# Output projections of two token groups in one pass over their weights, a weight ring of four whole blocks, and the first two block products taken two at once

## The chip, the core and the metric

The kernel runs on one core of a Trainium2 chip. The core has five engines: PE (TensorE) multiplies matrices, DVE (VectorE) and ACT (ScalarE) work on tiles of 128 partitions, POOL (GpSimd) does tile work that needs no PSUM, and SP (SyncE) issues most of the loads. The engines run side by side, each works its own list in order, and they wait for one another by semaphores. The metric is the device time of one execution in microseconds (us); lower is better.

## The reference, cut to what matters

One inference step of a hybrid decoder with two layers: layer 0 mixes tokens with a causal convolution, layer 1 with the RWKV-7 recurrence; each is followed by an MLP with a squared ReLU. The model width is 1024, the MLP's is 4096. There are 1040 prompt tokens (16 of them meta tokens) and 8 decode tokens, 1048 columns in all, in float32.

```python
def _sqrelu_mlp(h, w_in, w_out):
    return jnp.square(jax.nn.relu(h @ w_in)) @ w_out
...
def _rwkv7(h, shift_prev, S0, x_mix, w_r, w_k, w_v, w_o, ...):
    ...
    S_final, ys = lax.scan(_wkv7_step, S0.astype(f32), xs)
    ...
    out = ((yn + bonus).astype(h.dtype) * g) @ w_o
    return out, h[:, -1], S_final.astype(S0.dtype)
...
def _trunk(h, ...):
    for i in range(DEPTH):
        hn = _rmsnorm(h, norm_mix[i])
        ...
        h = h + out
        h = h + _sqrelu_mlp(_rmsnorm(h, norm_mlp[i]), w_mlp_in[i], w_mlp_out[i])
    return (_rmsnorm(h, norm_final), ...)
```

The change touches `out = (...) @ w_o` of layer 1, and the beginning of layer 1's MLP.

## The kernel before

**A matmul is three.** Every dense product is made from `float32` operands that are cut into a high part, rounded to the fast format `fp32r`, and the low rest. `mm3` issues high x high, low weight x high activation, and high weight x low activation (lines 190 to 192). For a weight block of 128 partitions x 1024 columns, ACT makes the high part (a CAST, line 158) and POOL subtracts it from the raw block in four pieces of 256 columns to get the low part (line 165). Both stand between the load and PE. For an activation tile ACT casts and DVE (or POOL) subtracts (lines 141 and 142).

**Token groups.** Layer 1's columns are worked in three groups: group 0 has 328 columns, groups one and two (the second and the third) have 352 each. `wide` is 352. Group two holds the decode tokens too, so its input `z2` needs the end of `decode_step`, which is worked beside group 0's MLP.

**Output projection.** `mixer_out(g)` loads the group's `z`, cuts it, and loops over the 8 column blocks `m` of `w_o`: the product `oo{g}_{m}` is 24 matmuls (8 pieces of the inner dimension times three), then DVE adds it to the residual `h1` (line 1685), ACT squares the sum (line 273), and POOL or DVE gathers the squares (`acc_m`, line 284) for the next norm. Weights are asked for two blocks ahead. For group 0 a weight block is one pair of tiles out of a pool of 5 (`lf`, closed after group 0's MLP). For groups one and two a block is two half-block `unit`s out of a ring of 8 halves (`units`), so four blocks; each group loads, casts and subtracts all 8 blocks. Raw blocks land in tiles of tag `raw`.

**Side work.** While PE runs a list, `fill()` advances generators between its products. Group 0's list has the tail of the recurrence (its chunk state `fs`, lines 1308 and 1426), the decode step and the group norms as side work; group one's has `final(0)` (sums `acc_f`, their matmul `fs` at line 1706, transposes `pf` at line 1722); group two's has `later_half`, which makes the norm of group one (`st_m` at line 262, a reciprocal, eight `nf` at line 1798) and the first half of the activations of the block products.

**Block products.** The MLP of groups one and two together is a seven-product scheme of the Strassen kind over pairs `s` of MLP blocks. Its products are named "1" to "7"; each is 4 pieces x 3 = 12 matmuls into one of the banks V, Z, X, Y. "7" goes to Z, "3" to Y in the first two pairs, "1" and "2" to V and X. `weight(s, q)` makes the operand of product `q`, for most by DVE additions of quarter blocks (the tiles `s` of pool `mixw`). "7" and "3" need only group one's activations (`b2`), the others need group two's norm as well (`first_half`). The first two pairs, `s` = 0 and 1, are worked in an order of their own; the rest in steady turns with the second MLP matmul (`out`).

**What sets the order.** PE's list is in program order inside `in_order()`; the other engines' lists are ordered by the framework's scheduler with its own timeline, so a change at one place can move rows of DVE, ACT and POOL elsewhere. SBUF is handed out from stacked pools: a tile of a new pool waits for the last users of the address that it takes.

Of the kernel before, what the change touches and what calls it, by code (L numbers as in the profile page):

```python
# [8 lines left out]
F32 = mybir.dt.float32  # L9
# [37 lines left out]
def hybrid_step(tc, x_prompt, x_sample, state_conv, state_shift, state_wkv, meta_tokens,  # L47
# [10 lines left out]
    with ctx:  # L58
# [91 lines left out]
        def load_w(src, shape, name, eng_lo, tag="w", raw=None, keep=False):  # L150
# [43 lines left out]
        UK, UB = KT // 2, 8  # L194
# [18 lines left out]
        def unit(src, name, keep=False):  # L213

            hi, lo = (cur["units"].tile([P, UK, P], F32R, name=f"{name}_{q}", tag="u" + q, bufs=UB) for q in "hl")
            a, b = src.shape[1:]
            hv, lv = (t.rearrange("p k c -> p (k c)").rearrange("p (a b) -> p a b", a=a) for t in (hi, lo))
# [6 lines left out]
            return (hi, lo) if b == P else (hv, lv)  # L224
# [40 lines left out]
        def square_sums(n, name, place, engs, own=False):  # L265
# [5 lines left out]
            def add(k, src):  # L271
# [7 lines left out]
                else:  # L279
                    a = b = out[i][:, :n] if i < len(out) else None  # L280
                    if a is None:
                        out.append(stat(f"acc_{name}{i}", f"acc{i}", 1))
                        a, b = out[i][:, :n], first[i]
# [1358 lines left out]
        with ExitStack() as l1:  # L1642
            open_tmp(l1, N2, "2", 3, False)
            actp = pool(l1, "actp1", 1)
# [3 lines left out]
            lf = ctx.enter_context(ExitStack())  # L1648
            open_weights(lf, 0, {"w": 5}, "f")
# [9 lines left out]
            def mixer_out(g, actp, fill, add):  # L1659
                lo, n = G2[g]  # L1660
                h1 = hl[g]

                def block(m):
                    if not g:
                        return load_col(rwkv_w_o[0], m, f"wo{g}_{m}", nc.gpsimd, keep=m > 0)
                    raw = blocks_of(load_raw(col_src(rwkv_w_o[0], m), (KT, P), f"wo{g}_{m}"))
                    return [unit(raw[:, i * UK:(i + 1) * UK], f"wo{g}_{m}_{i}", m > 0) for i in range(2)]
                z = new_acts(actp, f"z{g}", cur["wide"])
                ws, per = [], 8 * P // n
                for p in range(0, KT, per):  # L1670
# [4 lines left out]
                    if p == 0:  # L1675
                        ws.append(block(0))
# [3 lines left out]
                ws.append(block(1))  # L1680
                for m in range(KT):
                    if m + 2 < KT:
                        ws.append(block(m + 2))
                    ps = dense(ws.pop(0), z, n, f"oo{g}_{m}", fill)
                    nc.vector.tensor_add(h1[:, m, :n], h1[:, m, :n], ps[:, :n])
                    add(m, h1[:, m, :n])
# [340 lines left out]
```

## Time and profile before

| what | value |
|---|---|
| three runs | 2664.55, 2668.51, 2669.19 us, median 2668.51 |
| profiled execution | 2664.08 us, span 2662.3 us, 1.8 us outside the span |
| mean granted clock of PE | 0.987 |
| busy share of the span | PE 97%, DVE 68%, POOL 60%, ACT 45% |
| group 0's projection starts | 1701.5 us |
| projection of group one starts, group two's ends | 2068.2 us, about 2146.7 us |
| second MLP matmul starts | 2202.9 us |

The profiled execution is 4.4 us below the median of the three runs. In the profile's lists of waits a row names the engine that waits, what it wanted to do, and who released it. In a timeline a row has the start and the length in us, the engine, the line, the operation, what it writes and reads, how many such instructions in a row, and in brackets the idle time ahead of it and its releaser. In a table by stretches of time the last three columns are PE's granted clock as a share of full speed, the busy share of the DMA engines, and GB/s.

### The profile page before, as it was taken

The page shows a single profiled execution, that of the slowest core. Times are in us where ns is not written, and L with a number is a line of the kernel's source. Part 1 is how long each engine was busy: PE and PEld are TensorE (multiplying, and loading weights), DVE is VectorE, ACT ScalarE, POOL GpSimd, SP SyncE. Part 2 cuts the span into 40 slices and gives each one's busy share as a digit, 9 for nine tenths or more (in the row PEclk, how much of TensorE's full clock was granted, in tenths as well). Part 3 has the DMA queues.
Part 4 walks back from the last instruction along what each step waited for, and adds up shares of the span by engine and source line. Part 5 has one row for each costly group of instructions (what it writes and reads, how often), then busy time and mean ns, then how long its engine had stood idle before and what let it go on. Part 6 is the DMA issues. An engine that isn't in the chain of part 4 may idle for free.

```text
span 2662.3 us, 51898 instructions
## 1 busy us (share of the span) xinstructions
PE 2571.5 (97%) x19764; PEld 2422.5 (91%) x19764; DVE 1820.4 (68%) x3723; ACT 1187.7 (45%) x2264; POOL 1589.1 (60%) x2170
## 2 busy tenths in 40 slices
PE   8999999999999999999999999889999979999998
PEld 8999999999999999777788877789999869999998
DVE  6999999997444344445758567676689586565655
ACT  5546445444544333333345545454543543333333
POOL 7677878877878876022112113465587786666662
PEclk9999999999999999999999999899999999999999
DMA  7663544554446543678777858958665522222221
GB/s 188 171 170 107 166 140 133 159 178 135 136 140 186 155 136 111 201 202 220 209 185 204 219 145 215 236 143 191 174 193 172 149 69 72 64 80 80 64 72 44
DMA packets 602062, 400.24 MB, mean 150 GB/s; under 512 B 96128, under 2 KB 548928, under 8 KB 601814
## 3 DMA queue, kind: packets, MB, share of 16 engines
q1 hardware_dynamic: 573764, 360.08, 48.9%
q0 software_dynamic: 8720, 26.35, 3.3%
q10 hardware_dynamic: 19330, 10.49, 1.4%
q8 instruction: 156, 2.56, 0.4%
q14 instruction: 92, 0.75, 0.1%
HBM read 338.94 MB, written 58.83 MB: 149 GB/s over the span
## 4 chain that ended last, share of the span: by engine, by line
PE 80%; DVE 11%; DMA 3%; POOL 2%; ACT 2%; issue 2%; ACTq 0%; SPq 0%; DVEq 0%; POOLq 0%
PE out L190 8%; PE out L192 8%; PE out L191 8%; PE ps_in L190 5%; PE ps_in L191 5%; PE ps_in L192 5%; PE pk L943 4%; PE pr L943 4%; PE pv L943 3%; PE V L192 1%; PE V L190 1%; PE V L191 1%; PE ps_o L192 1%; PE ps_o L190 1%; PE ps_o L191 1%
## 5 line engine op out<-in xcount | busy, mean ns | idle before, releaser
L165 POOL TENSOR_TENSOR wo_lo<-wo_raw,wo_hi 128x256 fp32r<-128x256 f32 x544 | 397.9, 763 | 122.8 <-ACT wo_hi L158 117.2
L165 POOL TENSOR_TENSOR wi_lo<-wi_raw,wi_hi 128x256 fp32r<-128x256 f32 x512 | 378.0, 771 | 106.8 <-ACT wi_hi L158 103.0
L563 DVE SCALAR_TENSOR_TENSOR cv<-u,wdw,cv 128x348 f32<-128x348 f32 (+2 forms) x720 | 377.6, 574 | 0.7
L190 PE MATMUL out<-hh,wo_hi 128*128 128x348 f32 (+2 forms) x1024 | 332.3, 324 | 8.8 <-DVE h L381 7.4
L190 PE MATMUL ps_in<-m_h,wi_hi 128*128 128x348 f32 (+2 forms) x1024 | 328.7, 321 | 0.0
L192 PE MATMUL ps_in<-m_l,wi_hi 128*128 128x348 f32 (+2 forms) x1024 | 327.2, 320 | 0.5 <-DVE m_l L309 0.5
L191 PE MATMUL ps_in<-m_h,wi_lo 128*128 128x348 f32 (+2 forms) x1024 | 326.8, 319 | 0.0
L191 PE MATMUL out<-hh,wo_lo 128*128 128x348 f32 (+2 forms) x1024 | 326.7, 319 | 0.0
L192 PE MATMUL out<-hl,wo_hi 128*128 128x348 f32 (+2 forms) x1024 | 326.6, 319 | 0.0
L381 DVE TENSOR_TENSOR h<-h,out 128x348 f32<-128x348 f32 (+2 forms) x512 | 253.3, 505 | 69.5 <-PE out L192 67.8
L158 ACT CAST wi_hi<-wi_raw 128x1024 fp32r<-128x1024 f32 x128 | 134.1, 1048 | 260.2 <-PE ps_in L192 108.5
L158 ACT CAST wo_hi<-wo_raw 128x1024 fp32r<-128x1024 f32 x136 | 142.4, 1048 | 196.1 <-PE ps_in L192 91.9
L223 POOL TENSOR_TENSOR wo_l<-wo_raw,wo_h 128x256 fp32r<-128x256 f32 x192 | 163.7, 877 | 73.1 <-ACT wo_h L218 69.0
L190 PEld LDWEIGHTS out<-hh,wo_hi 128*128 128x128 f32 x1024 | 193.2, 189 | 14.1 <-DVE h L381 10.0
L190 PEld LDWEIGHTS ps_in<-m_h,wi_hi 128*128 128x128 f32 x1024 | 192.7, 188 | 1.3
L191 PEld LDWEIGHTS out<-hh,wo_lo 128*128 128x128 f32 x1024 | 192.5, 188 | 0.8
L192 PEld LDWEIGHTS ps_in<-m_l,wi_hi 128*128 128x128 f32 x1024 | 192.1, 188 | 1.1 <-DVE m_l L309 0.7
L191 PEld LDWEIGHTS ps_in<-m_h,wi_lo 128*128 128x128 f32 x1024 | 192.6, 188 | 0.5
L192 PEld LDWEIGHTS out<-hl,wo_hi 128*128 128x128 f32 x1024 | 192.3, 188 | 0.0
L1940 DVE TENSOR_TENSOR h<-h,out 128x352 f32<-128x352 f32 x256 | 131.7, 516 | 85.4 <-PE out L192 85.1
L192 PE MATMUL out<-hl,wo_h 128*128 128x352 f32 x512 | 167.3, 327 | 4.3 <-DVE hl L142 4.3
L190 PE MATMUL out<-hh,wo_h 128*128 128x352 f32 x512 | 167.6, 327 | 0.2 <-ACT hh L141 0.2
(475 smaller groups left out, 6685.8 us busy)
## 6 DMA issues: line engine op xcount, KB each, us to landing
wi_raw<-in_w_mlp_in_dram SPq DMA_DIRECT2D x160, 512.0 KB
wo_raw<-in_w_mlp_out_dram SPq DMA_DIRECT2D x160, 512.0 KB
wk_raw<-in_rwkv_w_k_dram SPq DMA_DIRECT2D x32, 512.0 KB
wr_raw<-in_rwkv_w_r_dram SPq DMA_DIRECT2D x32, 512.0 KB
wv_raw<-in_rwkv_w_v_dram SPq DMA_DIRECT2D x32, 512.0 KB
d_ab<-ab POOLq DMA_DIRECT2D x32, 512.0 KB, 4.3
pg_raw<-in_conv_w_pw_dram SPq DMA_DIRECT2D x24, 512.0 KB
pa_raw<-in_conv_w_pw_dram SPq DMA_DIRECT2D x24, 512.0 KB
```

Of the source, the lines that this page charges most:

```text
L158: cast = nc.scalar.copy(hi[:, :a * b], raw[:, :a * b])
L165: eng_lo.tensor_sub(lo[:, cs], raw[:, cs], hi[:, cs].bitcast(F32))
L190: nc.tensor.matmul(ps, w[0], act[0], start=first, stop=False, skip_group_check=onto)
L191: nc.tensor.matmul(ps, w[1], act[0], start=False, stop=False, skip_group_check=onto)
L192: nc.tensor.matmul(ps, w[0], act[1], start=False, stop=last, skip_group_check=onto)
L223: nc.gpsimd.tensor_sub(lv[:, i:i + step], src[:, i:i + step], hv[:, i:i + step].bitcast(F32))
L381: total = nc.vector.tensor_add(hv[:, 4 * i + m, :], hv[:, 4 * i + m, :], ps[:, :n])
L563: nc.vector.scalar_tensor_tensor(acc[m][:, :n], ug[:, m, j:j + n], wdw[:, m, j:j + 1], acc[m][:, :n], op0=ALU.mult, op1=ALU.add)
L943: nc.tensor.matmul(ps[:, :n], w[:, k, :], act[k], start=k == 0, stop=k == KT - 1)
L1940: nc.vector.tensor_add(hl[g][:, m, :n], hl[g][:, m, :n], ps[:, :n])
```

## The change

1. One loop takes the projections of groups one and two: `oo1_m`, and then `oo2_{m-3}` (`LEAD` = 3). Each block of `w_o` is loaded, cast and subtracted once and used by both groups: 8 loads of 512 KB, 8 blocks' casts and 32 subtractions fewer.
2. The weight ring is opened early, ahead of `actp1`, as two pools: `wspf` with four block slots and `wsps` with one. Group 0 goes round all five; from group one on the four are the ring, and the fifth's tiles become the quarter-block tiles of `weight`. A block-product `unit` is half of a slot's pair of tiles.
3. The first two pairs are worked two at once: `product("7", 0, 1)` alternates between the two banks piece by piece, in the order 7, 3, 1, 2, 6, 4, 5, with the weights of "7" and "3" of both pairs asked for first. Where two products alternate and their weights lie in one slot, the ring of four holds both.
4. The squared ReLU moves from one DVE operation to two ACT ones (Relu, Square), and works in PSUM. The reciprocal of the joint MLP's norms is written into PSUM.

The diff, cut:

```diff
@@ weights @@
-            nb = cur["bufs"][tag]
-            hi = cur["wsp"].tile([P, 8 * P], F32R, name=f"{name}_hi", tag=tag + "h", bufs=nb)
-            lo = cur["wsp"].tile([P, 8 * P], F32R, name=f"{name}_lo", tag=tag + "l", bufs=nb)
+            if "slot" in cur:
+                hi, lo = cur["slot"](name)
+            else:
...
         def unit(src, name, keep=False):
-            hi, lo = (cur["units"].tile([P, UK, P], F32R, name=f"{name}_{q}", tag="u" + q, bufs=UB) for q in "hl")
+            if not cur.get("pair"):
+                cur["pair"] = [t[:, i * UK * P:(i + 1) * UK * P] for t in cur["slot"](name) for i in range(2)]
+            hi, lo = cur["pair"].pop(0), cur["pair"].pop(len(cur["pair"]) // 2)
@@ layer 1 @@
             open_tmp(l1, N2, "2", 3, False)
+            rings = [pool(l1, f"wsp{i}", 1) for i in "fs"]
             actp = pool(l1, "actp1", 1)
...
-            lf = ctx.enter_context(ExitStack())
-            open_weights(lf, 0, {"w": 5}, "f")
+            cur["ring"], cur["turn"] = (0, 0, 0, 0, 1), 0
+            def slot(name):
+                i = cur["ring"][cur["turn"] % len(cur["ring"])]
+                cur["turn"] += 1
+                return [rings[i].tile([P, 8 * P], F32R, name=f"{name}_{q}", tag="w" + q, bufs=(4, 1)[i]) for q in ("hi", "lo")]
+            cur["slot"] = slot
...
-            lf.close()
             cur["wide"] = wide
-            cur["units"] = pool(l1, "units", UB)
-            mixed_w = pool(l1, "mixw", 5)
...
-            with in_order():
-                mixer_out(1, actp, fill, add)
...
+            cur["ring"] = (0,)
...
-            fill, rest = filler(2 * KT, ([late_start(2), later_half(sums)], 2 + 2 * UK + 2))
-            add, sums = sums_of(2)
+            LEAD = 3
+            adds = {}
+            fill, rest = filler(3 * KT, ([late_start(4), final(0)], FB + 4))
+            fills = {1: fill, 2: fill}
             with in_order():
-                mixer_out(2, actp2, fill, add)
+                for g in (1, 2):
+                    adds[g] = sums_of(g, ("rsm", 2) if g == 2 else None)
+                ws = {}
+                zs = {1: load_z(1, actp, lambda: ws.update({0: wo_block(0, "")}))}
+                for m in (1, 2):
+                    ws[m] = wo_block(m, "")
+                for m in range(KT + LEAD):
+                    if m < KT:
+                        if m + 3 < KT:
+                            ws[m + 3] = wo_block(m + 3, "")
+                        wo_product(1, m, ws[m], zs[1], fills[1], adds[1][0])
+                    if m == 0:
+                        zs[2] = load_z(2, actp2)
+                    if m == KT - 1:
+                        for _ in rest:
+                            pass
+                        fills[2], rest = filler(2 * LEAD + 2, ([late_start(1), later_half(adds[1][1])], 2 * UK + 1))
+                    if m >= LEAD:
+                        wo_product(2, m - LEAD, ws.pop(m - LEAD), zs[2], fills[2], adds[2][0])
...
             def squared(c):
-                nc.vector.scalar_tensor_tensor(c, c, 0.0, c, op0=ALU.max, op1=ALU.mult)
+                nc.scalar.activation(c, c, AF.Relu)
+                nc.scalar.activation(c, c, AF.Square)
...
                 for k in range(UK):
-                    mm3(ps, block_of([w], k), [t[k][:, :n] for t in hi_lo[q]], first and k == 0, k == UK - 1, not first)
+                    for s, w in zip(sets, ws):
+                        mm3(held[s, tag], block_of([w], k), [t[k][:, :n] for t in hi_lo[q]], first and k == 0, k == UK - 1, not first)
+                for s in sets:
+                    landed(s, q, early)
...
-                product(0, "7", True)
+                for s in range(2):
+                    ahead.update({(s, q): weight(s, q) for q in "73"})
+                product("7", 0, 1, early=True)
                 first_half(sums)
-                product(0, "3", True)
-                for q in "73":
-                    product(1, q, True)
...
+                for q in "3126":
+                    product(q, 0, 1, early=True)
+                for q in "45":
+                    product(q, 0, 1)
```

Here `wo_product` is the body of the old loop over `m`, and `load_z` its beginning.

How instructions move, at three places. In these rows a name's trailing number tells one tile from the next, and brackets hold the engines and DMA queues whose semaphores the instruction waits for. First PE, around group one's product for block 4, before:

```order
L190 MATMUL ps_oo_3_24377<-z_h_24116,wo_3_1_h 128x352
L191 MATMUL ps_oo_3_24377<-z_h_24116,wo_3_1_l 128x352
L192 MATMUL ps_oo_3_24377<-z_l_24124,wo_3_1_h 128x352
L190 MATMUL ps_oo_4_24433<-z_h_24109,wo_4_0_h 128x352 [waits Activation_49]
L191 MATMUL ps_oo_4_24433<-z_h_24109,wo_4_0_l 128x352 [waits Pool_49]
L192 MATMUL ps_oo_4_24433<-z_l_24117,wo_4_0_h 128x352
```

and after, where `ps_oo_0` is group two's product for block 0:

```order
L193 MATMUL ps_oo_0_24423<-z_h_24219,wo_hi 128x352
L194 MATMUL ps_oo_0_24423<-z_h_24219,wo_lo 128x352
L195 MATMUL ps_oo_0_24423<-z_l_24227,wo_hi 128x352 [waits DVE_49]
L193 MATMUL ps_oo_4_24474<-z_h_24108,wo_hi 128x352 [waits Activation_49]
L194 MATMUL ps_oo_4_24474<-z_h_24108,wo_lo 128x352 [waits Pool_49]
L195 MATMUL ps_oo_4_24474<-z_l_24116,wo_hi 128x352
```

The last reader of block 0's slot, which block 4 takes over, now stands directly in front of block 4's first reader.

Second POOL, in group 0's projection, where its sum `acc_m` takes the square of block 4, before:

```order
L284 TENSOR_TENSOR acc_m_19632<-acc_m_19632,sq_4_19767 128x328 [waits Activation_49,Pool_49]
L1274 MEMSET ni_19306 128x32 [waits DMAHW6_49,DVE_49]
L1275 DMA d_p<-ni_19306 128x1024 [waits DMASW7_49,DVE_49,Pool_49]
L165 TENSOR_TENSOR wo_7_lo<-wo_7_raw,wo_7_hi 128x256 [waits DMAHW1_49,PE_49,Activation_49]
L165 TENSOR_TENSOR wo_7_lo<-wo_7_raw,wo_7_hi 128x256 x3
L165 TENSOR_TENSOR wi_0_0_lo<-wi_0_0_raw,wi_0_0_hi 128x256 [waits DMAHW5_49,PE_49,Activation_49]
L165 TENSOR_TENSOR wi_0_0_lo<-wi_0_0_raw,wi_0_0_hi 128x256 x3
L165 TENSOR_TENSOR wi_0_1_lo<-wi_0_1_raw,wi_0_1_hi 128x256 [waits DMAHW6_49,PE_49,Activation_49]
L165 TENSOR_TENSOR wi_0_1_lo<-wi_0_1_raw,wi_0_1_hi 128x256 x3
L165 TENSOR_TENSOR wi_0_2_lo<-wi_0_2_raw,wi_0_2_hi 128x256 [waits DMAHW7_49,Activation_49]
```

and after:

```order
L168 TENSOR_TENSOR wi_0_1_lo<-wi_0_1_raw,wi_0_1_hi 128x256 [waits DMAHW6_49,Activation_49,Pool_49]
L168 TENSOR_TENSOR wi_0_1_lo<-wi_0_1_raw,wi_0_1_hi 128x256 x3
L289 TENSOR_TENSOR acc_m_19635<-acc_m_19635,sq_4_19770 128x328 [waits Activation_49,Pool_49]
L168 TENSOR_TENSOR wo_7_lo<-wo_7_raw,wo_7_hi 128x256 [waits DMAHW1_49,Activation_49]
L168 TENSOR_TENSOR wo_7_lo<-wo_7_raw,wo_7_hi 128x256 x3
L168 TENSOR_TENSOR wi_0_0_lo<-wi_0_0_raw,wi_0_0_hi 128x256 [waits DMAHW5_49,Activation_49]
L168 TENSOR_TENSOR wi_0_0_lo<-wi_0_0_raw,wi_0_0_hi 128x256 x3
L1279 MEMSET ni_19306 128x32 [waits DMAHW3_49,DVE_49]
L168 TENSOR_TENSOR wi_0_2_lo<-wi_0_2_raw,wi_0_2_hi 128x256 [waits DMAHW7_49,Activation_49]
```

The memset that waits for DVE has moved from ahead of the subtractions of `wo_7` and of the first three blocks of the MLP to between the second and the third of what is left of them. On ACT, the cast of group 0's block 0 moves from behind the eight `z_h` casts to ahead of them.

Third PE, at the norm of group one (`st_m`), before, in group two's block 1:

```order
L191 MATMUL ps_oo_1_24684<-z_h_24571,wo_1_0_l 128x352
L192 MATMUL ps_oo_1_24684<-z_l_24579,wo_1_0_h 128x352
L262 MATMUL st_m_24697<-acc_m_24363,ones_d 128x352
L262 MATMUL st_m_24697<-acc_m_24419,ones_d 128x352
L262 MATMUL st_m_24697<-sq_6_24529,ones_d 128x352 [waits Activation_49]
L262 MATMUL st_m_24697<-sq_7_24557,ones_d 128x352 [waits Activation_49]
L190 MATMUL ps_oo_1_24684<-z_h_24572,wo_1_1_h 128x352
```

and after, in group two's block 4:

```order
L194 MATMUL ps_oo_4_24690<-z_h_24215,wo_lo 128x352
L195 MATMUL ps_oo_4_24690<-z_l_24223,wo_hi 128x352
L267 MATMUL st_m_24703<-acc_m_24368,ones_d 128x352
L267 MATMUL st_m_24703<-acc_m_24421,ones_d 128x352
L267 MATMUL st_m_24703<-sq_6_24630,ones_d 128x352
L267 MATMUL st_m_24703<-sq_7_24688,ones_d 128x352 [waits Activation_49]
L193 MATMUL ps_oo_4_24690<-z_h_24216,wo_hi 128x352
```

Between this norm and the first block product 156 matmuls stood before and 84 stand now. Between group two's norm and the first matmul of V, 36 stood before (Y, Z, Y) and 24 stand now (Y and Y, alternating).

More of the change, by code (lines that the diff above doesn't have):

```diff
@@ L1 @@
 from contextlib import ExitStack, nullcontext
-from itertools import chain
+from itertools import chain, cycle
 import concourse.bass as bass
@@ L263, in mean_bcast, with square_sums @@
             return ps
-        def square_sums(n, name, place, engs, own=False):
+        def square_sums(n, name, place, engs, own=False, tag=None):
             out, first = [], []
@@ L1657, in load_h, with load_z @@
                 nc.sync.dma_start(hl[g][:, :, :n], d_h[:, :, lo:lo + n])
-            def mixer_out(g, actp, fill, add):
+            def load_z(g, actp, after=lambda: None):
                 lo, n = G2[g]
[L1661 to L1667, printed above, removed]
                 z = new_acts(actp, f"z{g}", cur["wide"])
-                ws, per = [], 8 * P // n
+                per = 8 * P // n
                 for p in range(0, KT, per):
@@ L1675, in mixer_out @@
                     if p == 0:
-                        ws.append(block(0))
+                        after()
                     for i in range(some):
@@ L1859, in hybrid_step @@
             NS = DFF // (2 * P)
-            raws, sums_w, hid, held = {}, {}, {}, {}
+            raws, sums_w, hid, held, ahead = {}, {}, {}, {}, {}
+            spare = [rings[1].tile([P, 8 * P], F32, name=f"sw{q}", tag="w" + q) for q in ("hi", "lo")]
+            spare = [t[:, i * UK * P:(i + 1) * UK * P] for t in spare for i in range(2)]
+            spare.append(combp.tile([P, UK * P], F32, name="sw"))
+            mixed = cycle([t.rearrange("p (k c) -> p k c", k=UK) for t in spare])
             def weight(s, q):
@@ L1867, in weight @@
                     order = (4, 1, 2) if s == 0 else (1, 2, 4)
-                    made = {i: mixed_w.tile([P, UK, P], F32, name=f"s{i}_{s}", tag="s") for i in order}
+                    made = {i: next(mixed) for i in order}
                     s1, s2, s4 = (made[i] for i in (1, 2, 4))
@@ L1896, in product, with bank_of @@
+            def bank_of(q, early):
+                return "Y" if early and q == "3" else {"2": "X", "7": "Z", "4": "Z"}.get(q, "V")
+            def product(q, *sets, early=False):
+                ws = [ahead.pop((s, q), None) or weight(s, q) for s in sets]
+                tag = bank_of(q, early)
                 first = tag == "Y" or q in "127"
                 if first:
-                    held[s, tag] = bank(f"{tag}{s}", "mm" if tag == "Y" or early and s and tag == "Z" else tag)[:, :n]
-                ps = held[s, tag]
+                    for s in sets:
+                        held[s, tag] = bank(f"{tag}{s}", "mm" if tag == "Y" or early and s and tag != "V" else tag)[:, :n]
@@ L1984, in hybrid_step @@
                             out(s, m, G[0], ws[m // 2])
-                    product(s, q)
+                    product(q, s)
                     take(pend, o)
```

112 lines of the change are left out of this document (57 added, 55 removed).

## The prediction

> **What bounds the kernel now.** I read the page first, for the engine that is full and for the clock that it was granted.
>
> ```profile
> span 2662.3 us, 51898 instructions
> PE 2571.5 (97%) x19764; PEld 2422.5 (91%) x19764; DVE 1820.4 (68%) x3723; ACT 1187.7 (45%) x2264; POOL 1589.1 (60%) x2170
> PEclk9999999999999999999999999899999999999999
> ```
>
> PE is the bound, and the change leaves the number of its matmuls alone. So only two things can move the time: PE's idle gaps and stretches at a lower clock. Next I took the waits of PE alone from 1690 us (the start of group 0's output projection) to 2210 us (behind the early block products).
>
> ```profile
> PE A L1308 <- DVE fs L1426: 12.1, 2, 7.7
> PE V L192 <- DVE b_l L142: 8.8, 2, 7.7
> PE out L192 <- DVE hl L142: 3.5, 1, 3.5
> PE st_m L262 <- ACT sq L273: 3.4, 1, 3.4
> PE fs L1706 <- POOL acc_f L254: 3.0, 1, 3.0
> PE U L1400 <- DVE w L1386: 2.0, 1, 2.0
> PE ps_oo L191 <- POOL wo_l L223: 1.8, 2, 1.4
> PE ps_oo L191 <- POOL wo_lo L165: 1.6, 1, 1.6
> PE ps_oo L190 <- ACT wo_hi L158: 1.1, 1, 1.1
> PE ynd L1599 <- issue: 0.9, 1, 0.9
> ```
>
> The columns are total us, number of waits and the longest. No wait of the list names a DMA, though each of the 16 weight blocks of groups one and two is loaded, cast and subtracted by itself. The loads, casts and subtractions that the change drops are thus worth nothing by themselves; what counts is what else stands behind them. By stage (busy time of PE, PEld, DVE, ACT, POOL, then PE's clock):
>
> ```profile
> 2068.20:2146.70 78.50, 72.72 (x437) 69.62 (x437) 48.32 (x74) 39.37 (x86) 59.75 (x71) 0.98 0.53 145
> 2146.70:2202.90 56.20, 37.01 (x191) 32.89 (x190) 47.68 (x66) 28.25 (x59) 51.87 (x52) 0.91 0.21 65
> 2223.00:2323.00 100.00, 100.00 (x620) 100.00 (x619) 58.20 (x102) 34.84 (x67) 65.05 (x76) 1.00 0.25 74
> ```
>
> The first row is the projections of groups one and two, the second the early block products, the third the steady state behind them. There PE is full, at 100/620 = 0.161 us a matmul, so one w_o block for one group (24 matmuls) is 3.87 us. Squares that go from DVE to ACT cost nothing there, since ACT has 65 us of 100 free; that cover lasts as long as PE is full, and at the very end of the kernel, where PE waits for the last square, I add 0.5 (one ACT pass more, like the 0.55 of `sd_m` in a row below).
>
> **The ring's new wait.** The ring has four slots and group two runs three blocks behind group one. Block m+4 takes the slot of block m, whose last reader is group two's product m, and that stands on PE right ahead of group one's product m+4. So the cast of blocks 4 to 7 starts only when PE has nothing else left. Before, the same ring was read by one group at a time and blocks were cast two ahead. The price is a handoff from cast to subtraction to PE, which the trace shows once, at the start of group one:
>
> ```profile
> 2067.54 2.17 ACT L218 CAST wo_h<-wo_raw 128x512 fp32r<-128x512 f32 x4
> 2068.20 0.43 PE L190 MATMUL ps_oo<-z_h,wo_h 128*128 128x352 f32 x1 [0.22 <-ACT wo_h L218]
> 2068.31 1.88 POOL L223 TENSOR_TENSOR wo_l<-wo_raw,wo_h 128x256 fp32r<-128x256 f32 x2
> 2069.09 0.43 PE L191 MATMUL ps_oo<-z_h,wo_l 128*128 128x352 f32 x1 [0.47 <-POOL wo_l L223]
> ```
>
> and these are the mean of all such steps on the page:
>
> ```profile
> L165 POOL TENSOR_TENSOR wo_lo<-wo_raw,wo_hi 128x256 fp32r<-128x256 f32 x544 | 397.9, 763 | 122.8 <-ACT wo_hi L158 117.2
> L158 ACT CAST wo_hi<-wo_raw 128x1024 fp32r<-128x1024 f32 x136 | 142.4, 1048 | 196.1 <-PE ps_in L192 91.9
> ```
>
> From the start of the half-block cast to the first low product 2069.09 - 2067.54 = 1.55 us. A whole-block cast takes 1.05 instead of 2.17/4 = 0.54, which makes 2.06; one high product (0.16) runs meanwhile, and PE's release adds about 0.1. That is 2.0 us, four times: **+8.0**. Ends: 1.8 each if the subtraction takes its mean of 0.76 instead of 0.94 (+7), 3.0 each if ACT or POOL are held by a square or a sum in front (+12). Queued behind the waiting cast on ACT are squares of both groups, which only the norms need. A fifth wait: group two's first product now stands early, and its activations need the decode step's stores; I take +1.1, the cast wait of 1.1 in the table being the nearest (0 to 3).
>
> Does the clock fall too? These slices give PE's busy time, its clock and DMA:
>
> ```profile
> 1696.00:1698.00 2.00, 2.00 (x31) 0.50 1.05 383
> 1704.00:1706.00 2.00, 2.00 (x9) 0.50 1.15 337
> 1757.10:1763.00 5.90, 5.84 (x28) 0.50 1.22 228
> 1948.00:1950.00 2.00, 1.85 (x12) 1.00 0.51 107
> 2080.00:2084.00 4.00, 3.89 (x23) 0.63 0.26 55
> ```
>
> After the single 2.0 us wait of 1948 (in MLP code, among full work) the clock stayed at 1.00; after the 2.0 us of `U`, and after 1.1 and 1.6 us close together, it was 0.50. The new waits are single, with 7.7 us of full work between, which is nearest to 1948, so I take no drop. The Trainium skill ("TensorE: Matmul & The Clock Gate", HAM oscillation — how this bites in real kernels) puts the limit at idle gaps of about 3.4 us, by which the sum stays as it is; the two 0.50 slices after shorter gaps differ from that, and the measurement decides.
>
> **What leaves the projections.** The ring is open from the start, so blocks 0 and 1 of group one are cast while group 0's MLP still runs: the waits for `wo_h` and `wo_l` at the start, (0.2 + 0.5), and the later 1.4 go. The 3.0 of `fs` waited for `acc_f` on POOL, queued behind late subtractions of w_o; those now come earlier, and with the gap goes the low clock behind it, 4 x 0.37 = 1.5. The 0.9 of `ynd` goes. Sum -(0.2 + 1.8 + 3.0 + 1.5 + 0.9) = **-7.4**; ends -8.6 and -4 (`fs` finds another late square). Projections together: 8.0 + 1.1 - 7.4 = +1.7.
>
> **The early products.** Group one's norm (`st_m`) is now issued in the middle of group two's block 4, with 84 matmuls = 13.5 us up to the first product; before, in the middle of block 1, with 156. These rows are the chain behind `st_m` for group one, then for group two:
>
> ```profile
> L289 ACT ACTIVATE sd_m<-st_m,eps_t x1: 554/554/554, 2119.2 to 2119.2; 128x352 f32<-128x352 f32 x1
> 2122.48 6.49 DVE L1798 SCALAR_TENSOR_TENSOR nf<-h,pvec,rs_m 128x352 f32<-128x352 f32 x8
> 2139.82 1.06 DVE L142 TENSOR_TENSOR b_l<-t,b_h 128x352 fp32r<-128x352 f32 x1
> 2155.98 2.35 DVE L291 RECIPROCAL rs_m<-sd_m 128x352 f32<-128x352 f32 x1 [4.29 <-ACT sd_m L289]
> 2158.37 7.82 DVE L1798 SCALAR_TENSOR_TENSOR nf<-h,pvec,rs_m 128x352 f32<-128x352 f32 x8
> 2167.95 1.25 DVE L142 TENSOR_TENSOR b_l<-nf,b_h 128x352 fp32r<-128x352 f32 x1
> ```
>
> From 2119.2 to the end of the last split is 21.7 us, about 22 from the norm's last matmul. The pair of products uses its four splits one after another over 3.87 us, so it ends near 22.0 instead of 13.5 + 3.9 = 17.4: **+4.5** (2 if less weight mixing stands between, 9 if the chain is as much slower as 7.82 is beside 6.49). What is late next is group two's norm: its 3.4 us wait for a square goes, as the pair has covered it (**-3.4**). Behind it V waits for 2169.2 (2167.95 + 1.25) - 2156.0 = 13.2 us of reciprocal, eight `nf` and a split. Its cover shrinks from 36 matmuls to 24 (+1.9), one more subtraction comes ahead (+0.6), and I expect `nf` at the 0.81 (6.49/8) of group one instead of 0.98 (7.82/8), since POOL, at 92% in this stage, has 32 subtractions fewer in front of it (-1.3): **+1.2** (-3 to +3). The eight squares that leave DVE, busy 85% there, cost at most 0.81 each, like `nf`; I take half of that, 3.2 us, and half of it on the path, by the 1.5 us wait of X: **-1.6** (-3 to 0). Together +0.7.
>
> **Group 0.** Its weights take slots that are free early, and ACT casts block 0 ahead of the eight `z_h` casts instead of behind them. These are the last four of those casts and the block's cast before:
>
> ```profile
> 1692.18 1.56 ACT L141 CAST z_h<-zr 128x328 fp32r<-128x328 f32 x4
> 1700.44 1.99 ACT L158 CAST wo_hi<-wo_raw 128x1024 fp32r<-128x1024 f32 x2 [0.45 <-ACT vt L1093]
> ```
>
> PE then waited 1.1 and 1.6 us for it. Both go, and half of each microsecond at the 0.50 of 1704 behind them; but the `z_h` casts, 8 x 1.56/4 = 3.1 us, now come later. I take **-3.0**; ends -8 (the 2.0 of `U` and part of the first 4.4 us `A` wait go too) and +2 (the activations become the late ones).
>
> The largest wait is elsewhere:
>
> ```profile
> 1745.17 2.80 POOL L165 TENSOR_TENSOR wo_lo<-wo_raw,wo_hi 128x256 fp32r<-128x256 f32 x4
> 1747.94 8.20 POOL L165 TENSOR_TENSOR wi_lo<-wi_raw,wi_hi 128x256 fp32r<-128x256 f32 x12
> 1746.87 9.63 DVE L284 TENSOR_TENSOR acc_m<-acc_m,sq 128x328 f32<-128x328 f32 x1 [1.79 <-ACT sq L273]
> 1756.43 0.68 DVE L1426 TENSOR_TENSOR fs<-S,wc 128x512 f32<-128x512 f32 x1
> 1757.16 0.58 PE L1308 MATMUL A<-xa,bk 64*128 64x128 f32 x2 [7.69 <-DVE fs L1426]
> ```
>
> A sum of half a microsecond took 9.63 us on DVE, and ended when POOL's 16 subtractions, run without a pause, had ended; `fs` stood behind it and PE behind `fs`. The Trainium skill ("GPSIMD Engine Reference", Specifications) has POOL share its SBUF interfaces with DVE operations of two SBUF inputs, which fits this row. In the new order one block's subtractions stand ahead of POOL's own `acc_m`, eight behind it, and then a memset that waits for DVE. So the run is at most 8 x 0.71 = 5.7 us, and it starts earlier against the sum. I take the wait as gone with the half clock behind it: 7.7 + 5.9/2 = **-10.7**. If the sum still meets the run it is held 4 us less and 2.6 of the 7.7 remain (-8); if nothing changes, 0.
>
> **Sum.** 1.7 + 0.7 - 3.0 - 10.7 + 0.5 = -10.8, on the profiled execution's 2664.1: 2653.3. The median of the three runs shown lies 4.4 above that execution; taking half of it as what a new median would show gives 2655.5, **2655**.
>
> **Rivals.**
> - *The ring draws the clock down.* Each of the four waits ends in half clock, as after `U`, for a time between the 2 us of those slices and the 5.9 us of 1757, say 4: 4 x 2.0 = +8.0, 2663. The 0.50 of 1704 is for it, the 1.00 of 1948 against. Chance 0.15. The Trainium skill ("TensorE: Matmul & The Clock Gate", A second HAM failure mode) tells of frequent short idling that makes the clock swing, a rule that speaks against this change.
> - *The shut-out stays or moves.* DVE is held once for about 9.6 us on the path: 2655 + 10.7 = 2666, no change that can be told. For it: POOL still runs eight in a row. Against: the new pause. Chance 0.20.
> - *Slower: the shut-out doubles.* DVE is held twice, behind group 0's runs and in the chain ahead of V, where PE has nothing else: 2655 + 21.4 = 2676. It decides from two events of 9.4 us on. For it: ACT and POOL do blocks 4 to 7 in bursts; against: one such event in the whole trace. Chance 0.12.
> - *The later half is bare:* the first pair waits 9 instead of 4.5, 2660: the same dead time in another place. Chance 0.10.
>
> **How the numbers follow.** The sum as it stands has 0.43, with its own range of 2643 to 2661. A measurement of this kernel tells about 0.2% (5.3 us) from no change. Slower: 0.12 and 0.02 of mixtures, 0.14. Faster: 0.43, 0.10 and 0.08 of the clock's 0.15, which lies on the edge, 0.61. Same: 0.20 and 0.07, less the 0.02 of mixtures, 0.25. The range reaches from 2642 (group 0 at -8, V at -3, the squares at -3, the ring at +7, which makes 2655 - 5.0 - 4.2 - 1.4 - 1.0 = 2643, and a microsecond of the offset) to 2674, just short of the doubled shut-out.
>
> **What will show it.** Four PE waits of about 2 us for `wo`, with 7.7 us of work between, at clock 1.00; no `fs` wait of 7 us near 1757, and no DVE sum above 3 us; a first pair that waits 2 to 6 us on `b_l`; V starting within 3 us of 2169 less what group 0 saved. I am wrong if the ring's waits are over 3 us each or leave the clock at 0.50, or if DVE is held anywhere else on the path.

## The result, and the profile after

The changed kernel's median is 2645.05 us (2641.04 to 2650.53) beside 2667.6 us of the kernel before; the ratio is 0.9918, with a 95% interval of 0.9895 to 0.9941. In a second series it was 2646.33 us, 0.9920 (0.9905 to 0.9935). The forecast was 2655, with 2642 to 2674: faster as said, by 22.6 us instead of 13.5. The profiled execution took 2647.91 us, 16.2 less than that of before. The page of the changed kernel:

```profile
span 2646.1 us, 51757 instructions
PE 2565.4 (97%) x19764; PEld 2416.1 (91%) x19764; DVE 1775.7 (67%) x3673; ACT 1218.8 (46%) x2340; POOL 1534.5 (58%) x2138
PEclk9999999999999999999999999999999989999999
```

PE issues the same 19764 matmuls and has 10 us less idle time and 6 us less busy time; part of the latter goes with a higher mean clock (0.987 to 0.989), part with the steady state, which is taken up below. Its longest waits over the same part of the program as in the prediction (total us, number, longest; the first row lies in group 0's MLP, and its counterpart of before, 4.9 us, is not in the prediction's list):

```profile
PE out L193 <- DVE h L386: 5.8, 5, 2.0
PE A L1313 <- DVE fs L1431: 5.3, 2, 3.4
PE ps_oo L193 <- ACT wo_hi L161: 4.5, 4, 1.1
PE V L195 <- DVE b_l L142: 3.9, 1, 3.9
PE V L193 <- ACT b_h L141: 2.9, 1, 2.9
PE out L193 <- ACT hh L141: 2.7, 1, 2.7
PE U L1405 <- DVE w L1391: 2.0, 1, 2.0
PE ps_oo L194 <- POOL wo_lo L168: 1.5, 4, 0.4
PE pf L1740 <- ACT ot L1743: 1.2, 1, 1.2
PE Z L195 <- DVE b_l L142: 1.2, 2, 1.0
```

The wait of 7.7 for `fs` is gone (its two waits are now 3.4 and 1.9), and so are those of `acc_f` and `st_m`. New are four waits for `wo_hi` with four for `wo_lo` directly behind them: the ring's. Now the stages, as busy time in stretches. These two rows are the changed kernel's projections of groups one and two, from the first matmul to the last, and its early products up to the first matmul of the second MLP product; behind them stands the row of before for the early products, within the same ends (that for the projections stands in the prediction). The columns are the stretch and its length, PE, PEld, DVE, ACT and POOL with their instructions, granted clock, DMA share and GB/s.

```profile
2059.80:2141.10 81.30, 74.05 (x438) 70.48 (x437) 38.69 (x71) 30.36 (x63) 32.25 (x38) 0.96 0.33 94
2141.10:2184.80 43.70, 34.29 (x179) 30.70 (x178) 35.55 (x54) 25.38 (x58) 31.67 (x34) 0.88 0.17 50
```

The kernel before, early products:

```profile
2146.50:2196.50 50.00, 34.48 (x178) 30.78 (x177) 41.44 (x57) 25.78 (x54) 45.67 (x45) 0.90 0.20 63
```

POOL's busy time in the projections fell from 59.8 to 32.3 us and their DMA share from 0.53 to 0.33, and yet they became longer. Halving the work on the weights bought nothing there. The early products became 6.3 us shorter. From one and the same matmul shortly ahead of group 0's projection (the last of `vt`, at about 1690 us) to the first of group one's it is 378.1 us before and 369.6 after; from the first `out` behind the early products to the last matmul 459.9 and 455.1. So the 16 us are -8.5 in group 0, +3.0 in the projections, -6.3 in the early products and -4.9 behind them; the missing 0.5 lies outside these stages.

### The profile page after: what moved, and what is told of

It reads as the page before. It is cut to its first block, busy times and chain, and to the rows that moved or that the text cites. A ratio compares the mean times of both kernels' runs of the same rounds, so it can differ in the third digit from the quotient of the medians.

```text
span 2646.1 us, 51757 instructions
## 1 busy us (share of the span) xinstructions
PE 2565.4 (97%) x19764; PEld 2416.1 (91%) x19764; DVE 1775.7 (67%) x3673; ACT 1218.8 (46%) x2340; POOL 1534.5 (58%) x2138
## 4 chain that ended last, share of the span: by engine, by line
PE 81%; DVE 10%; DMA 3%; issue 2%; POOL 2%; ACT 2%; SPq 0%; ACTq 0%; DVEq 0%; POOLq 0%
PE out L193 8%; PE out L195 8%; PE out L194 8%; PE ps_in L193 5%; PE ps_in L194 5%; PE ps_in L195 5%; PE pk L948 4%; PE pr L948 4%; PE pv L948 3%; PE V L195 1%; PE V L193 1%; PE V L194 1%; PE ps_o L195 1%; PE ps_o L193 1%; PE ps_o L194 1%
## 5 line engine op out<-in xcount | busy, mean ns | idle before, releaser
L168 POOL TENSOR_TENSOR wo_lo<-wo_raw,wo_hi 128x256 fp32r<-128x256 f32 x576 | 425.4, 771 | 153.5 <-ACT wo_hi L161 152.6
L193 PE MATMUL out<-hh,wo_hi 128*128 128x352 f32 (+2 forms) x1328 | 432.8, 326 | 12.3 <-DVE h L386 8.3
L195 PE MATMUL out<-hl,wo_hi 128*128 128x352 f32 (+2 forms) x1328 | 426.9, 322 | 0.3 <-DVE hl L142 0.3
L194 PE MATMUL out<-hh,wo_lo 128*128 128x352 f32 (+2 forms) x1328 | 427.1, 322 | 0.0
L193 PEld LDWEIGHTS out<-hh,wo_hi 128*128 128x128 f32 x1328 | 252.1, 190 | 17.6 <-DVE h L386 10.8
L194 PEld LDWEIGHTS out<-hh,wo_lo 128*128 128x128 f32 x1328 | 251.7, 189 | 0.8
L195 PEld LDWEIGHTS out<-hl,wo_hi 128*128 128x128 f32 x1328 | 251.1, 189 | 0.6 <-DVE hl L142 0.6
L373 DVE SCALAR_TENSOR_TENSOR ps_in<-ps_in,rs_m 128x348 f32<-128x348 f32 (+2 forms) x128 | 66.4, 520 | 135.2 <-PE ps_in L195 135.0
L1125 POOL DMA_DIRECT2D d_n<-n x32 | 24.4, 763 | 189.5 <-DVE n L1115 93.7
L948 PE MATMUL pk<-mx,wk_raw 128*128 128x256 f32 (+2 forms) x512 | 124.4, 395 | 2.1 <-DVE n L1115 1.9
```

The costliest lines, as they stand in the source:

```text
L168: eng_lo.tensor_sub(lo[:, cs], raw[:, cs], hi[:, cs].bitcast(F32))
L193: nc.tensor.matmul(ps, w[0], act[0], start=first, stop=False, skip_group_check=onto)
L194: nc.tensor.matmul(ps, w[1], act[0], start=False, stop=False, skip_group_check=onto)
L195: nc.tensor.matmul(ps, w[0], act[1], start=False, stop=last, skip_group_check=onto)
L373: nc.vector.scalar_tensor_tensor(s, s, 0.0, rs()[:, :n], op0=ALU.max, op1=ALU.mult)
L948: nc.tensor.matmul(ps[:, :n], w[:, k, :], act[k], start=k == 0, stop=k == KT - 1)
```

## The experiments

Theory A: the gain comes from the place of the ring, which is open early, and the single pass over the weights is worth little either way. Rival B: the single pass, with half the loads, casts and subtractions, is the gain. Stages in us from one profiled execution each, by the starts of PE's matmuls; the two rows of the changed kernel show how far two executions of one kernel can differ, most of all in the projections:

| kernel | median us | ratio to before (95%) | group 0 | projections | early products | rest |
|---|---|---|---|---|---|---|
| before | 2667.6 | 1 | 378.1 | 78.3 | 50.0 | 459.9 |
| changed | 2645.05 | 0.9918 (0.9895-0.9941) | 369.6 | 81.3 | 43.7 | 455.1 |
| changed, again | 2646.33 | 0.9920 (0.9905-0.9935) | 368.9 | 76.8 | 44.2 | 455.8 |
| place only | 2639.18 | 0.9885 (0.9870-0.9901) | 366.5 | 69.9 | 44.7 | 458.9 |
| two passes | 2636.28 | 0.9875 (0.9861-0.9888) | 369.2 | 69.9 | 46.7 | 453.6 |
| singles | 2646.75 | 0.9915 (0.9901-0.9928) | 366.6 | 79.6 | 46.1 | 453.4 |
| five slots | 2642.57 | 0.9896 (0.9881-0.9912) | 369.0 | 70.2 | 52.2 | 457.5 |
| lead of two | 2639.73 | 0.9895 (0.9880-0.9909) | 366.6 | 71.5 | 49.3 | 453.2 |
| two passes, singles | 2634.22 | 0.9876 (0.9860-0.9893) | 368.9 | 69.9 | 44.6 | 455.1 |
| reciprocal in SBUF | 2652.45 | 0.9948 (0.9931-0.9965) | 369.5 | 84.6 | 47.4 | 454.9 |

**Place only.** The ring as changed; the joint loop, the pairs and the square on ACT are undone, and the sums that are squared lie in SBUF again.

```diff
-            for m in range(KT + LEAD): ...          # the joint loop
+            mixer_out(1, actp, fill, add)
+            mixer_out(2, actp2, fill, add)
-                product("7", 0, 1, early=True)      # and the other pairs
+                product("7", 0, early=True)         # singles, in the order of before
-                nc.scalar.activation(c, c, AF.Relu)
-                nc.scalar.activation(c, c, AF.Square)
+                nc.vector.scalar_tensor_tensor(c, c, 0.0, c, op0=ALU.max, op1=ALU.mult)
```

(Not all else is undone: the norms' reciprocal stayed in PSUM, a point that comes back below, groups one and two kept whole-block casts, and the weights of "7" and "3" are still asked for first.)

> Only the early place of the weight ring is kept: the two projections are worked one after the other again, each with its own loads, the early products one at a time, and the square is back on DVE. Theory A (the gain is group 0's: its weights start sooner and DVE's sum is no longer shut out): 11 to 15 us below the kernel before. Rival B (the gain comes from halving the loads, casts and subtractions of w_o): within 4 us of the kernel before, since that part is undone here. By A there is no VectorE sum above 3 us near 1747 us and PE's wait for fs there is about 2 us instead of 7.7.

It gained 29 us, twice what theory A said, and B is out: without the single pass the gain is not lost. Theory A's sign is there, no VectorE operation of more than 3 us near 1747. But it put the gain in group 0 alone, and the table has 11.6 us of it there, 8.4 in the projections and 5.3 in the early products.

**Two passes.** Only the joint loop is undone, as in the first three lines above.

> The changed kernel with the projections of groups one and two one after the other again (16 blocks loaded, cast and subtracted instead of 8); ring, pairs and squares as changed. Theory A: the four waits for the reused slots go, and the waits of a late second pass come back; the time is within 5 us of the changed kernel. Rival B (the single pass is what gains): 10 us or more above the changed kernel.

2636.28: 9 us below the changed kernel, more than the 5 that theory A allowed, and on the other side of what B said. So the single pass is a loss, which neither had said. The projections take 69.9 us in both kernels with two passes, 8.4 less than before with the same number of loads and subtractions. The best of them, the two changes undone together (last of this list), has them in this row:

```profile
2055.70:2125.50 69.80, 69.34 (x438) 67.20 (x436) 44.90 (x74) 36.18 (x68) 51.13 (x61) 1.00 0.59 162
```

And the waits of the same stretch, all of them:

```profile
PE ps_oo L194 <- POOL wo_lo L168: 0.3, 1, 0.3
```

One wait of 0.3 us is left, in the place-only kernel as well. What I had booked under "leaves the projections", 7.4 us, thus comes with the ring as it is placed now (and the whole-block casts that go with it), and needs no single pass.

**Singles.** The pairs undone, as in the second hunk above, the rest as changed.

> The changed kernel with the first two block products taken one at a time in the old order. Theory A (the chain of reciprocal, norm and splits on VectorE sets this stage, the order of the products little): within 3 us of the changed kernel. Rival C (the pairs cover the norms better, which is where the stage gained 6.6 us): 5 to 7 us above the changed kernel.

2646.75 beside 2645.05 and 2646.33: the pairs are worth nothing that shows, and theory A holds for them.

**Five slots.** `cur["ring"] = (0,)` moved from ahead of the joint projections to behind them.

> The changed kernel with all five slots in the ring during the joint projections instead of four, so that a block is cast one product earlier. Theory A: the four waits of 1.5 us for wo go, and the two stretches of half clock behind them (3.4 us): 6 to 9 us below the changed kernel. Rival D (the time only moves on to the first pair, which waits for the norm of group one anyway): within 2 us of it.

The ring's waits went, and the projections came to 70.2 us. But the fifth slot's tiles are the quarter-block tiles of the first products, now late, and the first wait in the list behind the projections says what came instead:

```profile
PE Z L193 <- ACT wi_hi L223: 4.7, 1, 4.7
```

The early products took 52.2 us instead of 43.7: rival D was right on most of the gain. 2642.57 is 2.5 us below the changed kernel, and the intervals of the two overlap, so no difference is shown.

**Lead of two.** `LEAD = 2`, four slots.

> The changed kernel with group two two blocks behind group one instead of three, four slots as changed. Block m+4 then finds block m's slot free two products (7.7 us) ahead of its use. If the four waits for wo and their half clock are what the single pass costs (11 us against two passes in the new ring, by the traces), they go, and the time comes to that of two passes, about 2637, 7 to 10 us below the changed kernel. Rival: the time is given back at the first pair as with five slots, within 3 us of the changed kernel; there the first pair waited 4.7 us for a cast, here the fifth slot is free and it should wait only for its activations, though the norm of group one now stands 24 matmuls closer to it, which alone would add up to 4 us.

2639.73, 5.3 below the changed kernel and so between the two forecasts; the intervals of the two kernels overlap. The projections fall to 71.5, without a wait for `wo`. A fifth slot and a shorter distance both take the waits away, so the direct neighbourhood of last reader and next writer was their cause. 5 us are given back as the expectation feared, at the first pair, which now waits for group one's norm:

```profile
PE Z L195 <- DVE b_l L142: 4.6, 1, 4.6
```

**The sum on POOL, in the kernel before.** It separates the 9.6 us sum from all else.

```diff
-                                   (nc.gpsimd, nc.vector))
+                                   (nc.gpsimd, nc.gpsimd if g == 0 else nc.vector))
```

> The kernel before, with both halves of group 0's sum of squares on POOL, so that VectorE has no sum in front of the state update near 1747 us. If VectorE's 9.6 us sum behind POOL's run of 16 subtractions is what delayed fs and PE, PE's 7.7 us wait and the half clock behind it go: 7 to 11 us below the kernel before. Rival: some other VectorE operation of two SBUF inputs is shut out in its place, and the wait stays at 5 us or more.

2661.14, ratio 0.9976 (0.9967 to 0.9986): 6.8 us faster, just under what I expected. The rival had its part, since another VectorE operation of two SBUF inputs was held, for as long as POOL's run lasted (two operations in the first row, of which the first took 8.4; POOL's own sum stands at the end of the run):

```profile
1747.16 9.13 DVE L1429 TENSOR_TENSOR sv<-fs,sw 64x512 f32<-64x512 f32 x2 [0.18 <-PE Y L1418]
...
1743.78 2.13 POOL L165 TENSOR_TENSOR wo_lo<-wo_raw,wo_hi 128x256 fp32r<-128x256 f32 x3
1745.87 8.32 POOL L165 TENSOR_TENSOR wi_lo<-wi_raw,wi_hi 128x256 fp32r<-128x256 f32 x12
1754.15 0.86 POOL L284 TENSOR_TENSOR acc_m<-acc_m,sq 128x328 f32<-128x328 f32 x1
```

This one stood behind `fs` instead of ahead of it, so PE's longest wait there was 3.7 instead of 7.7.

**Paired slots, in the kernel before.** Units as halves of double tiles, the pool in its old place.

> The kernel before, with two half-block weight units placed in one tile of double size, as in the changed kernel; the pool stays where it was. In the steady state a matmul took 0.1618 us before and 0.1609 in the changed kernel and in all four variants so far. If the layout of the units does that, it is 0.1609 here; if the place of the pool or of the tiles beside it does, 0.1618. The time of the whole changes by 2 us at most.

2665.52, ratio 0.9990 (0.9979 to 1.0001), and 0.1618 us a matmul as before. (The rates here are counted by the matmuls that start between 2300 and 2500 us: 1236 and 1243.) The layout of the units is not what makes the steady state 0.6% quicker; what does is open.

**The changed kernel again.**

> The changed kernel itself again, so that the variants have it with more runs. 2641 to 2651 as measured before. If the single pass costs what the traces say (about 11 us of waits and half clock in the projections, of which some 3 come back in the early products), its median stays 6 to 11 us above that of two passes in the new ring (2636); by the rival, that the gap is chance of few runs, it comes within 3 us of that.

2646.33, 10 us above two passes, and the intervals do not meet (0.9905 to 0.9935 and 0.9861 to 0.9888): the difference is no chance of few runs. This second trace also settles a question on the clock, below.

**Two passes with singles.** Both hunks undone, the square on ACT.

> Two passes in the new ring with the early products one at a time, and the square on ACT: the candidate for the best version. If neither the order of the products nor the engine of the square matters, it lies between the two versions measured at 2636 and 2639, within 3 us of either; if the pairs help behind two passes, it is over 2640.

2634.22, the lowest median of all: 33 us below the kernel before, and 11 below the changed one. It lies 2 us under the lower of the two, not between them, but it can't be told from two passes with pairs (0.9876 beside 0.9875), nor, by its interval, from place only (0.9885). So neither the order of the products nor the engine of the square shows in the time.

**The reciprocal in SBUF.**

```diff
-                nc.vector.reciprocal(ps[:, :n], rs[:, :n])
+                nc.vector.reciprocal(rs[:, :n], rs[:, :n])
...
-                ... vec("norm_mlp", KT + k), ps[:, :n], ...
+                ... vec("norm_mlp", KT + k), rs[:, :n], ...
```

> The changed kernel with the reciprocal of the joint MLP's norms kept in SBUF instead of PSUM, so that the eight nf of each norm read both tensors from SBUF, as in the kernel before. In the changed kernel all sixteen nf took 0.57 to 0.58 us, also while POOL subtracted; before 0.57 to 1.07. If the PSUM operand is what keeps them apart from POOL, the nf that meet POOL's subtractions take about 1.05 again, group two's eight take 6 to 8 us instead of 4.0, and the early products lose 1 to 4 us. Rival: they are short because POOL is idle there, since the weights come earlier; then they stay at 0.58 and the time is the same within 2 us.

2652.45, 6 to 7 us slower than the two medians of the changed kernel. The sixteen `nf` of each kernel follow (shortest, median and longest in ns). The kernel before:

```profile
L1798 DVE SCALAR_TENSOR_TENSOR nf<-h,pvec,rs_m x16: 574/1046/1069, 2122.5 to 2165.1; 128x352 f32<-128x352 f32 x16
```

The changed kernel:

```profile
L1809 DVE SCALAR_TENSOR_TENSOR nf<-h,pvec,st_m x16: 569/576/581, 2131.1 to 2156.2; 128x352 f32<-128x352 f32 x16
```

With the reciprocal in SBUF again:

```profile
L1809 DVE SCALAR_TENSOR_TENSOR nf<-h,pvec,sd_m x16: 570/1046/1272, 2135.0 to 2164.0; 128x352 f32<-128x352 f32 x16
```

And in the changed kernel POOL was at work beside them, so its being idle is no explanation:

```profile
2152.76 4.02 DVE L1809 SCALAR_TENSOR_TENSOR nf<-h,pvec,st_m 128x352 f32<-128x352 f32 x8
...
2154.23 1.42 POOL L228 TENSOR_TENSOR wi_lo<-swlo,wi_hi 128x256 fp32r<-128x256 f32 x2 [6.55 <-ACT wi_hi L223]
2155.60 1.42 POOL L228 TENSOR_TENSOR wi_lo<-sw,wi_hi 128x256 fp32r<-128x256 f32 x2
```

With both tensors in SBUF an `nf` takes about twice as long while POOL subtracts (1.05, at most 1.27); with one in PSUM it takes 0.58 whatever POOL does. Group two's eight took 6.5 us in this variant, as expected. PE's wait at V was 7.5 us and is 3.9 in the changed kernel; these are the variant's waits for activations in the early products:

```profile
PE V L195 <- DVE b_l L142: 7.5, 1, 7.5
PE V L193 <- ACT b_h L141: 2.9, 1, 2.9
PE Z L195 <- DVE b_l L142: 2.5, 3, 1.3
PE Z L193 <- ACT b_h L141: 0.6, 1, 0.6
```

The early products account for 3.7 of the difference between the traces (3.2 beside the changed kernel's second trace). 3.3 more lie in the projections: 2.3 of them are PE's busy time at a lower clock (0.92 beside 0.96), which the next section takes up, and 1.2 a longer wait of `pf` (2.4 beside 1.2). So 3.2 to 3.7 us is what these traces show the operand's place to be worth. Place only has the reciprocal in PSUM too, so its 29 us are not the ring's alone.

## Why the prediction was right, and where not

The sum on the profiled execution was -10.8 and the measured difference is -16.2. Its four stages were out by +5.2 in group 0, +1.3 in the projections, -7.0 in the early products and -5.4 behind them. Errors of both signs cancel in part, so that the time falls into the range is in part luck. By its steps:

- **The ring's new wait: right in place, number and kind, a third too large.** Four waits, each behind group two's product, at 1.5 us instead of 2.0. The first of them, changed kernel:

```profile
2084.47 1.04 ACT L161 CAST wo_hi<-wo_raw 128x1024 fp32r<-128x1024 f32 x1 [0.77 <-PE ps_oo L195]
...
2085.57 0.43 PE L193 MATMUL ps_oo<-z_h,wo_hi 128*128 128x352 f32 x1 [1.14 <-ACT wo_hi L161]
2086.37 0.43 PE L194 MATMUL ps_oo<-z_h,wo_lo 128*128 128x352 f32 x1 [0.37 <-POOL wo_lo L168]
...
2085.59 2.80 POOL L168 TENSOR_TENSOR wo_lo<-wo_raw,wo_hi 128x256 fp32r<-128x256 f32 x4 [8.70 <-ACT wo_hi L161]
```

  From the cast's start to the low product it is 1.90 us. I had 2.06 from the handoff at 2068, where POOL's subtractions ran at 0.94 beside a busy VectorE, while here they take 2.80/4 = 0.70; the high product covers 0.43 of it by PE's rows, where I took 0.16. The fifth wait, for group two's activations, forecast at 1.1, did not come; a wait of 1.2 for `pf` did, in the first trace and not in the second.
- **The clock behind those waits: no drop was forecast, and both cases happened.** Two places behind waits in the first trace (stretch, length, PE, then clock, DMA share and GB/s):

```profile
2098.00:2100.00 2.00, 2.00 (x9) 0.52 0.13 38
2118.00:2120.00 2.00, 1.97 (x8) 0.64 0.00 0
```

  The same places in the second, and its whole stretch of projections:

```profile
2098.00:2100.00 2.00, 2.00 (x14) 1.00 0.60 172
2118.00:2120.00 2.00, 2.00 (x14) 1.00 0.87 239
2080.00:2120.00 40.00, 33.95 (x204) 1.00 0.46 138
```

  The waits were 1.5 us in both executions. In the first the second and the fourth ended in 3.4 us at clock 0.50, which costs 1.7 us each; in the second none did. That, with the 1.2 of `pf`, is why the projections took 81.3 and 76.8. With four such waits the singles had one such drop, and the kernel with the reciprocal in SBUF had three stretches of low clock there. The rival of the clock thus had 3.4 of its 8.0 us in one execution of this kernel and nothing in the other. The Trainium skill ("TensorE: Matmul & The Clock Gate", Part 1: The HAM clock gate) says that the activity window runs freely and does not begin with the work; by that, where a wait falls in it is chance, and these two traces agree. That 1.5 us of idling can be enough differs from the 3.4 us that the Trainium skill puts as the limit in the section "HAM oscillation — how this bites in real kernels" of the same page.
- **What leaves the projections: right, but not the single pass's doing.** Forecast -7.4. In the changed kernel the waits of 5.8 us in all for `fs`, `wo_l`, `wo_h` and `ynd` are gone, and so is the low clock behind `fs` (3.4 us at 0.50, 1.7 us), together 7.5. With two passes in the same ring they are gone too (78.3 to 69.9). The forecast had credited the open ring for this, but it had not asked what the ring gives when the single pass is left out: against two passes in it the single pass costs 76.8 - 69.9 = 6.9 us without low clock and 11.4 with it.
- **Early products: forecast +0.7, measured -6.3.** Two terms were mis-sized: the first pair waited 1.2 instead of the 4.5 forecast, and V's waits fell by 2.0 (8.8 to 3.9 + 2.9) where 1.2 more were forecast. (The 3.4 of `st_m` and the 1.5 of X went, as forecast.) Behind both stands `nf`. I took it at 0.81 us each, from group one's chain, and gave POOL's lighter load as the reason; it took 0.50 a step (4.02/8; the operations overlap a little, one alone is 0.58), because its second tensor had moved to PSUM. That is one line of the change, named in its fourth point, that I had costed at nothing. `nf` is 3.8 us shorter in group two's chain (7.82 to 4.02) and 2.5 in group one's (6.49 to 4.01). With the reciprocal back in SBUF V waits 7.5 + 2.9 us, which is 1.6 more than before and near the 1.2 forecast, and the first pair 2.5 + 0.6. So the operand's place is worth 3.6 at V and 1.9 of the 3.3 at the first pair (other waits and the clock take 1.8 of that back, which leaves the 3.7 by which the stage differs); why that pair waits 3.1 and not 4.5 even without it stays open. The Trainium skill ("GPSIMD Engine Reference", Key points) says that POOL shares its SBUF interfaces with VectorE and contends with operations of two SBUF inputs; the `nf` rows agree with that, at 1.05 with two and 0.58 with one. I had cited the rule for the long sum, and not asked which of the change's own operations lost a second SBUF input.
- **Group 0: forecast -13.7, measured -8.5** (-9.2 in the second trace). The start gained 5.3 at the first wait of `A` for `fs` (1715.66 to 1710.48, with the executions 0.15 apart ahead of it), more than the 3.0. At the second one 1.85 of the 7.7 remain, where I took it as gone; at the end of the projection PE was 13.2 us ahead (11.2 in the second trace). The shut-out is gone, as forecast, but not for the reason given:

```profile
1745.53 0.85 DVE L289 TENSOR_TENSOR acc_m<-acc_m,sq 128x328 f32<-128x328 f32 x1
...
1741.78 2.87 POOL L168 TENSOR_TENSOR wo_lo<-wo_raw,wo_hi 128x256 fp32r<-128x256 f32 x4
1744.61 3.03 POOL L168 TENSOR_TENSOR wi_lo<-wi_raw,wi_hi 128x256 fp32r<-128x256 f32 x4
...
1747.03 1.16 PE L1313 MATMUL A<-xa,bk 64*128 64x128 f32 x14 [1.85 <-DVE fs L1431]
```

  The sum did meet POOL's run of eight, in its middle, and took 0.85 us. That POOL runs without a pause is therefore not enough to shut VectorE out. In the three traces with a long shut-out VectorE had stood idle just ahead (1.79 in the kernel before, 0.18 with the sum on POOL, and 1.50 with paired slots, where the sum took 9.66 us), and here it had not. But idling is not what it takes: in two passes with singles VectorE worked up to a subtraction of two SBUF inputs, which took 2.83 us instead of 0.5 and ended just behind a POOL run, of which these are the last four:

```profile
2172.62 2.83 DVE L142 TENSOR_TENSOR hl<-c,hh 128x352 fp32r<-128x352 f32 x1
...
2172.30 1.41 POOL L228 TENSOR_TENSOR wo_lo<-wo_raw,wo_hi 128x256 fp32r<-128x256 f32 x2
2173.66 1.41 POOL L228 TENSOR_TENSOR wo_lo<-swlo,wo_hi 128x256 fp32r<-128x256 f32 x2
```

  What decides whether an operation is held stays open. Of the 13.2 us, 4.7 went again in group 0's MLP (2.0 in the second trace), more than half of it in low clock after waits that the kernel before had at clock 1.00: its 2.0 us at 1948 us, and one near 2055 that grew from 0.5 to 1.4.
- **Behind the early products: forecast +0.5, measured -4.9.** I had costed the steady state at nothing, because it has no waits. Before:

```profile
2300.00:2500.00 200.00, 200.00 (x1238) 200.00 (x1237) 119.08 (x206) 72.09 (x139) 133.73 (x154) 1.00 0.25 74
```

  After:

```profile
2300.00:2500.00 200.00, 200.00 (x1245) 200.00 (x1244) 108.22 (x187) 90.67 (x183) 120.22 (x154) 1.00 0.25 75
```

  PE is full in both and gets through 7 more matmuls in 200 us, 0.6%, which is 2.3 us over the steady state. Place only has the rate of the changed kernel (0.1609 us) with the squares on VectorE, and the paired slots have that of before, so neither of these does it, and the cause stays open. The other 2.6 us lie at both ends of the stage, in waits and low clock. One of the waits bears on the forecast: I added 0.5 at the very end for ACT's second pass, but the 0.8 us that PE waited there for the last split is gone with the squares on ACT, while place only, with them on VectorE, still has it (0.9).

## What to carry to other kernels

Before two passes over the same weights are merged, look at what PE waits for: to drop loads, casts and subtractions that never end a wait bought nothing here, and a shared ring with only one slot more than the distance between its two readers (four slots, three blocks) put a bare handoff into each turn. With one slot more, or one step less of distance, the handoff went, and part of what it freed was waited for at the next place. When a change takes an operand of a VectorE operation out of SBUF, cost that line by itself wherever POOL works beside it. And a change of several parts is worth undoing part by part even when it wins: here the ring and the reciprocal's new place gave as much as the whole or more, and the versions without the headline part were some 10 us better.

## What the runs showed of the hardware

- A VectorE operation with two SBUF inputs can be held until a run of POOL subtractions ends: 8.4 to 9.7 us in three traces, with 12 to 14 POOL operations beside it, and 2.8 us in two more, with four beside it, where such operations otherwise took 0.5 to 1.1. A similar one met a run of 8 in its middle and took 0.85.
- A VectorE operation on 128x352 in `float32` with two SBUF tensors took 0.57 us alone and 1.05 beside POOL's subtractions; with one of the two tensors in PSUM it took 0.57 to 0.58 beside them too.
- The same 1.5 us of idling left TensorE's clock at 1.00 in one execution and, in two cases of four, brought it to 0.50 for 3.4 us in another of the same kernel.
- Full steady states with the same matmuls and no wait ran at 0.1618 and 0.1609 us a matmul, the one in the kernel before and its two variants, the other in the changed kernel and all of its variants; why is not known.
